# Expert routing spread over more steps, its table lookup moved from GpSimd to VectorE, and the low weight parts given to one engine per stage

## The chip, the cores and the metric

The program runs on 1 core of one Trainium2 chip. The metric is device time in microseconds (us) of one execution; less is better. TensorE does the matrix products, VectorE and GpSimd elementwise work, ScalarE activations and casts, and SyncE's queue issues nearly all DMAs.

## The reference

Three networks run one after the other on 256 positions of width 1024, all in float32. The change lies in the first network alone, in its two product-key expert layers (`peer_ffn`), cut here to what is computed:

```python
def peer_ffn(h, wq, k1, k2, u_tab, v_tab):
    def block(xb):                                   # 128 positions
        q = (xb @ wq).reshape(PEER_BLOCK, PEER_HEADS, 2, PEER_HALF)
        s1 = jnp.einsum('phd,kd->phk', q[:, :, 0], k1).astype(jnp.float32)
        s2 = jnp.einsum('phd,kd->phk', q[:, :, 1], k2).astype(jnp.float32)
        v1, i1 = lax.top_k(s1, PEER_TOPK)            # 16 of 128 keys
        v2, i2 = lax.top_k(s2, PEER_TOPK)
        cand = (v1[..., :, None] + v2[..., None, :]) # 256 sums per head
        cand_id = i1[..., :, None] * N_KEYS + i2[..., None, :]
        top_s, top_pos = lax.top_k(cand, PEER_TOPK)
        eid = jnp.take_along_axis(cand_id, top_pos, axis=-1)
        g = jax.nn.softmax(top_s, axis=-1)
        act = jax.nn.gelu(jnp.einsum('pd,phkd->phk', xb, u_tab[eid]))
        return jnp.einsum('phk,phkd->pd', g.astype(xb.dtype) * act, v_tab[eid])
    return lax.map(block, h.reshape(-1, PEER_BLOCK, D)).reshape(B, S, D)
```

There are 8 heads, 128 keys per half and so 16384 experts. The kernel gathers no expert rows. It multiplies all positions by the whole of U (128 chunks of 128 experts), builds a dense gate matrix G from the routing, and multiplies gelu(U h) times G by the whole of V.

## The kernel before

**Low parts.** Each float32 weight tile is split into a high part (rounded, ScalarE, line 164) and a low part (tile minus high part, line 168), and each product is three matmuls: high by high, high by low, low by high (`mm3`, lines 179 to 181). The third one needs the low part. `wunit` loads 512 KB into a `raw` buffer (6 of them), and writes both parts into the buffers `hl` (8 of them, so four tiles in flight in this stage). Its argument `lo` says who makes the low part: "v" is VectorE, "g" is GpSimd. Without an argument it follows the letters of `self.pat`.

**`peer_route`** runs once for each layer. It first multiplies by `wq`, eight groups of two tiles: three in `lead` together with the norm, then five in a loop that calls `advance(2.5)` before each. `ev_q` and `keys` make the key scores. Then `LAG + SPILL` = 91 chunks of U follow, each by one call of `step`: `advance(budget)`, then `u_chunk` (24 matmuls into one PSUM tile, then a gelu on ScalarE, line 1258), then the delayed products of the gate matrix. The first 40 activations are written to HBM, 51 stay in the `act` buffers (52).

**Routing** is a generator, `routing()`: 32 calls of `top_half` (VectorE's top-8 instructions over 128 scores, for 8 heads, 2 halves and 2 position blocks), then `route(th)` for each block of 128 positions. `route` adds the two lists to 54 candidates, takes the best 16 (lines 1107 to 1111), makes the softmax (an Exp on ScalarE, line 1117), turns positions into two indices A and B (lines 1125 to 1150), and looks both up in the index lists: a one-hot comparison `oh` (line 1157), a product with the list on GpSimd (line 1161) and a sum (line 1163), four times for each block. After three transposes on TensorE (line 1169) come 16 steps that build one-hot tiles `ob` (line 1184) and weighted ones `oa` (line 1190); TensorE multiplies these (line 1200, 16 products for each step), ScalarE evacuates (line 1204), and SyncE stores 1 MB of G (line 1207) for every two steps. The tiles `tr` that `ob` and `oa` read have two buffers, one block's worth; `ob` and `oa` have three each.

**Pacing.** Each `yield` of the generator gives the cost of what it has just emitted, and `advance` runs it until the costs have used up the budget. With the costs before, routing's last piece falls on step 64 of the 91; with those after, on step 83 (added up from the yields and budgets in the code). In what order an engine gets its instructions is settled when the program is built: a scheduler places the instructions in program order where they are ready by its own estimate, and may place a later one in a gap. On the chip each engine's order is then fixed.

**Who makes U's low parts.** Before: GpSimd for three chunks of every five, with the larger budget (2.6), else VectorE (1.5).

**`peer_value`** runs the other 37 chunks of U beside the products with V. Its first one needs `gr`, a read of G (line 1295) behind all its stores, then a product on GpSimd (line 1305).

Of the kernel before, what the change touches and what calls it, by code (L numbers as in the profile page):

```python
# [10 lines left out]
F32 = mybir.dt.float32  # L11
F32R = mybir.dt.float32r
BF16 = mybir.dt.bfloat16
F16 = mybir.dt.float16
# [6 lines left out]
P = 128  # L21
# [8 lines left out]
LAG = 51  # L30
SPILL = 40
# [21 lines left out]
MIX_BG = (0, 2, 4, 6, 8, 8)  # L53
MODS = ((1, 0, 2), (4, 3), (5,))
OH_COST = 1.3
BUDGET = (1.5, 2.6)
PAT_MIX = "ggv"
LEAD_LO = "vg"
SQ_POOL = 4
# [48 lines left out]
class Kern:  # L108
# [935 lines left out]
    def peer_route(self, l, nm):  # L1044
        hs = nm.xs
        nc, a = self.nc, self.a
        v = nc.vector
# [22 lines left out]
        def top_half(hd, s):  # L1070
            for th in range(2):
                for sd in range(2):
                    sj = s[:, th * 2 + sd]
                    Vt, It = V[th][sd], I[th][sd]
                    w = self.t([P, P], F32, "r")
                    v.max(out=Vt[:, hd, 0:8], in_=sj)
                    v.max_index(It[:, hd, 0:8], Vt[:, hd, 0:8], sj)
                    v.match_replace(w, Vt[:, hd, 0:8], sj, -3.0e38)
                    v.max(out=Vt[:, hd, 8:16], in_=w)
                    v.max_index(It[:, hd, 8:16], Vt[:, hd, 8:16], w)  # L1080
                    yield 1.0


        self.n += 1
# [3 lines left out]
        def route(th):  # L1088
            V1, V2 = V[th]
            If = []  # L1090
            for sd in range(2):
                t = self.t([P, 8, 16], F32, "r")
                v.tensor_copy(t, I[th][sd])
                If.append(t)
            cand = self.t([P, 8, 54], F32, "cand")
# [8 lines left out]
            for hd in range(8):  # L1104
                c = cand[:, hd]
                w = self.t([P, 54], F32, "r")
                v.max(out=TS[:, hd, 0:8], in_=c)
                v.max_index(PI[:, hd, 0:8], TS[:, hd, 0:8], c)
                v.match_replace(w, TS[:, hd, 0:8], c, -3.0e38)
                v.max(out=TS[:, hd, 8:16], in_=w)  # L1110
                v.max_index(PI[:, hd, 8:16], TS[:, hd, 8:16], w)
                if hd % 2:
                    yield 1.2

            g = self.t([P, 8, 16], F32, "r")
            v.tensor_sub(g, TS, TS[:, :, 0:1].broadcast_to([P, 8, 16]))
# [20 lines left out]
            v.tensor_scalar(u2, p, 37.0, None, op0=ALU.is_ge)  # L1137
            stt(u2, p, 40.0, u2, op0=ALU.is_ge, op1=ALU.add)
            stt(u2, p, 43.0, u2, op0=ALU.is_ge, op1=ALU.add)
            yield 1.2  # L1140
            stt(B, e16, -16.0, p, op0=ALU.mult, op1=ALU.add)
            stt(B, e24, -8.0, B, op0=ALU.mult, op1=ALU.add)
            stt(B, u1, -5.0, B, op0=ALU.mult, op1=ALU.add)
# [4 lines left out]
            v.tensor_add(A, A, e24)  # L1148
            v.tensor_add(A, A, u1)
            v.tensor_add(A, A, u2)  # L1150
            yield 1.8
            res = []
            for sel, tab in ((A, If[0]), (B, If[1])):
                ids = self.t([P, P], F32, "r")
                for hf in range(2):
                    oh = self.t([P, 4, 16, 16], BF16, "oh")
                    v.tensor_tensor(
                        oh.rearrange("p h k j -> p (h k) j"),
                        sel[:, hf * 64:hf * 64 + 64, None].broadcast_to([P, 64, 16]),
                        self.iota[:, None, 0:16].broadcast_to([P, 64, 16]), op=ALU.is_equal)  # L1160
                    nc.gpsimd.tensor_mul(oh, oh, tab[:, hf * 4:hf * 4 + 4, None, :].broadcast_to([P, 4, 16, 16]))
                    yield 1.1
                    v.tensor_reduce(ids[:, hf * 64:hf * 64 + 64], oh.rearrange("p h k j -> p (h k) j"),
                                    axis=AX.X, op=ALU.add)
                    yield 1.1
                res.append(ids)
            pt = self.ps("acc")
            for i, src in enumerate((g.rearrange("p h k -> p (h k)"), res[0], res[1])):
# [42 lines left out]
        def routing():  # L1211
            for s_hd in range(8):
                yield from top_half(s_hd, ss.pop(s_hd))
            for th in range(2):
                yield from route(th)

        ss = {}
        pend = []
        late = [[]]
        gen = routing()  # L1220
# [2 lines left out]
        def advance(budget):  # L1223
            self.debt += budget
            while self.debt > 0:
                try:
                    self.debt -= next(gen)
                except StopIteration:
                    return False
            return True  # L1230
# [4 lines left out]
        ss[1] = keys(1)  # L1235
        if LEADS > 2:
            ss[2] = keys(2)
        for g in range(LEADS, 8):
            advance(2.5)
            self.lin(wq, [g], hs, ev_q)  # L1240
            ss[g] = keys(g)

        acts = {}
        uw = {}
        st = {"u": 0}

        def u_chunk():
            i = st["u"]
            if i >= P:
                return  # L1250
            st["u"] += 1
            w = self.wload(a["U"][l, i // 2][:, (i % 2) * D:(i % 2) * D + D], NK, P,
                           lo="g" if i < LAG + SPILL and i % 5 < 3 else "v")
            p = self.ps()
            for k in range(NK):
                self.mm3(p[:, :S], *w[k], *hs[k], k == 0, k == NK - 1)
            t = self.t([P, S], F32, "act")
            nc.scalar.activation(t, p[:, :S], AF.Gelu_apprx_tanh)
            if i < SPILL:
                nc.sync.dma_start(Sd[i], t)  # L1260
            else:
                acts[i] = t
# [8 lines left out]
            return more or bool(pend) or any(late)  # L1271

        for i in range(LAG + SPILL):
            step(BUDGET[i % 5 < 3])
        while step(4.0):
            pass

        return u_chunk, acts, Gd, Sd

# [906 lines left out]
```

## Time and profile before

| | us |
|---|---|
| median of 3 runs | 3950.95 |
| lowest and highest run | 3948.46 and 3953.46 |
| the profiled execution's own time | 3954.35 |
| its span in the profile | 3952.5 |
| its mean granted TensorE clock | 0.97 |

The profiled execution is 3.4 us longer than the median of the runs shown, and 1.85 us of it lie outside the span. The engines' busy times over the span are 3712.5 us for TensorE's matmuls, 2832.6 us for VectorE, 1915.8 us for ScalarE and 1226.6 us for GpSimd. The two stages that the change touches begin with `wq` at about 200 and 1220 us; their 91 chunks of U run from about 248 to 594 us and from about 1268 to 1614 us. The page of the profile has a strip of 40 slices, about 99 us each, in which each digit is a busy share in tenths.

### The profile page before, as it was taken

The page shows a single profiled execution, that of the slowest core. Times are in us where ns is not written, and L with a number is a line of the kernel's source. Part 1 is how long each engine was busy: PE and PEld are TensorE (multiplying, and loading weights), DVE is VectorE, ACT ScalarE, POOL GpSimd, SP SyncE. Part 2 cuts the span into 40 slices and gives each one's busy share as a digit, 9 for nine tenths or more (in the row PEclk, how much of TensorE's full clock was granted, in tenths as well). Part 3 has the DMA queues.
Part 4 walks back from the last instruction along what each step waited for, and adds up shares of the span by engine and source line. Part 5 has one row for each costly group of instructions (what it writes and reads, how often), then busy time and mean ns, then how long its engine had stood idle before and what let it go on. Part 6 is the DMA issues. An engine that isn't in the chain of part 4 may idle for free.

```text
span 3952.5 us, 75873 instructions
## 1 busy us (share of the span) xinstructions
PE 3712.5 (94%) x30282; PEld 3626.1 (92%) x30282; DVE 2832.6 (72%) x5231; ACT 1915.8 (48%) x2900; POOL 1226.6 (31%) x922
## 2 busy tenths in 40 slices
PE   5888999999989799999999979999999998899998
PEld 4787999999979799999999979999899998789998
DVE  7899746676868976555667687675876768967665
ACT  4444544444454355444444434444554445755453
POOL 3335462133432545312424661121221212501100
PEclk8898999999999899999999989999999999999999
DMA  7545667796733477767764534558444553444452
GB/s 248 200 145 185 250 240 268 259 316 232 260 132 126 134 266 252 243 209 259 246 211 172 192 117 144 187 177 234 157 162 178 182 183 120 157 171 166 160 202 93
DMA packets 288435, 774.48 MB, mean 196 GB/s; under 512 B 25296, under 2 KB 117968, under 8 KB 283984
## 3 DMA queue, kind: packets, MB, share of 16 engines
q1 hardware_dynamic: 286496, 767.82, 56.7%
q8 instruction: 237, 3.88, 0.4%
q10 hardware_dynamic: 1584, 1.81, 0.1%
q14 instruction: 118, 0.97, 0.1%
HBM read 721.20 MB, written 48.27 MB: 195 GB/s over the span
## 4 chain that ended last, share of the span: by engine, by line
PE 65%; DVE 14%; DMA 2%; issue 2%; ACT 2%; POOL 1%; DVEq 0%; ACTq 0%; POOLq 0%; SPq 0%
PE mm L179 11%; PE mm L181 11%; PE mm L180 11%; PE acc L180 9%; PE acc L179 9%; PE acc L181 9%; DVE hl L168 2%; DMA raw<-in_ada 1%; DVE act L1399 1%; DVE hx L168 1%; DVE oa L1190 1%; DMA raw<-in_fg 1%; DVE M L1831 1%; DVE ob L1184 1%; DVE t L1739 1%
## 5 line engine op out<-in xcount | busy, mean ns | idle before, releaser
L168 DVE TENSOR_TENSOR hl<-raw,hl 128x512 fp32r<-128x512 f32 (+1 forms) x962 | 974.7, 1026 | 595.8 <-ACT hl L164 594.7
L164 ACT CAST hl<-raw 128x1024 fp32r<-128x1024 f32 x860 | 901.2, 1049 | 889.2 <-PE acc L180 396.2
L181 PE MATMUL mm<-h,hl 128*128 128x256 f32 x3688 | 1056.5, 287 | 60.4 <-POOL hl L168 32.2
L179 PE MATMUL mm<-h,hl 128*128 128x256 f32 x3688 | 1066.4, 289 | 1.6 <-DVE act L1859 1.2
L180 PE MATMUL mm<-h,hl 128*128 128x256 f32 x3688 | 1053.4, 286 | 0.3
L181 PEld LDWEIGHTS mm<-h,hl 128*128 128x128 f32 x3688 | 713.7, 194 | 67.5 <-POOL hl L168 34.4
L179 PEld LDWEIGHTS mm<-h,hl 128*128 128x128 f32 x3688 | 714.7, 194 | 5.7 <-issue 2.6
L180 PEld LDWEIGHTS mm<-h,hl 128*128 128x128 f32 x3688 | 714.5, 194 | 1.3 <-DVE h L586 0.9
L168 POOL TENSOR_TENSOR hl<-raw,hl 128x1024 fp32r<-128x1024 f32 x164 | 434.6, 2658 | 498.6 <-ACT hl L164 457.5
L181 PE MATMUL acc<-cc,hl 128*128 128x256 f32 x2048 | 579.2, 283 | 2.1 <-DVE hl L168 2.0
L179 PE MATMUL acc<-cc,hl 128*128 128x256 f32 x2048 | 578.9, 283 | 0.5 <-DVE x L1288 0.5
L180 PE MATMUL acc<-cc,hl 128*128 128x256 f32 x2048 | 579.0, 283 | 0.0
L168 DVE TENSOR_TENSOR hx<-raw,hx 128x512 fp32r<-128x512 f32 x558 | 425.4, 780 | 116.1 <-ACT hx L164 113.1
L1305 POOL TENSOR_TENSOR t<-act,gr 128x256 f32<-128x256 f32 x256 | 281.4, 1132 | 575.2 <-DMA gr<-G 465.7
L179 PE MATMUL mm<-h,hx 128*128 128x256 f32 x1464 | 415.6, 284 | 0.4 <-ACT hx L164 0.4
L181 PE MATMUL mm<-h,hx 128*128 128x256 f32 x1464 | 412.3, 282 | 0.8 <-POOL hx L168 0.6
L180 PE MATMUL mm<-h,hx 128*128 128x256 f32 x1464 | 412.9, 282 | 0.0
L164 ACT CAST hx<-raw 128x1024 fp32r<-128x1024 f32 x314 | 328.7, 1047 | 147.4 <-PE mm L180 73.5
L181 PEld LDWEIGHTS acc<-cc,hl 128*128 128x128 f32 x2048 | 389.7, 190 | 2.7 <-DVE hl L168 2.7
L179 PEld LDWEIGHTS acc<-cc,hl 128*128 128x128 f32 x2048 | 389.9, 190 | 0.7 <-DVE x L1288 0.7
L180 PEld LDWEIGHTS acc<-cc,hl 128*128 128x128 f32 x2048 | 389.7, 190 | 0.0
L754 POOL TENSOR_TENSOR t<-t,act 128x256 f32<-128x256 f32 x110 | 115.4, 1049 | 680.5 <-DVE t L753 641.0
(494 smaller groups left out, 7323.7 us busy)
## 6 DMA issues: line engine op xcount, KB each, us to landing
raw<-in_fg SPq DMA_DIRECT2D x264, 512.0 KB, 4.4
raw<-in_U SPq DMA_DIRECT2D x256, 512.0 KB, 4.5
raw<-in_V SPq DMA_DIRECT2D x256, 512.0 KB, 4.4
raw<-in_fd SPq DMA_DIRECT2D x132, 512.0 KB, 4.1
raw<-in_w SPq DMA_DIRECT2D x88, 512.0 KB, 4.0
G<-s SPq DMA_DIRECT2D x32, 1024.0 KB, 6.5
gr<-G SPq DMA_DIRECT2D x32, 1024.0 KB, 8.0
mr<-in_ada SPq DMA_DIRECT2D x56, 512.0 KB, 5.8
```

The costliest lines, as they stand in the source:

```text
L164: nc.scalar.copy(hi, raw)
L168: (nc.gpsimd if lo == "g" else nc.vector).tensor_sub(w, rw, h.bitcast(F32))
L179: mm(out, lhsT=wh, rhs=xh, start=start, stop=False, **kw)
L180: mm(out, lhsT=wh, rhs=xl, start=False, stop=False, **kw)
L181: return mm(out, lhsT=wl, rhs=xh, start=False, stop=stop, **kw)
L754: nc.gpsimd.tensor_mul(pr, u, r)
L1184: v.tensor_tensor(oh, self.iota2[:, None].broadcast_to([P, 8, P, 2]), ids[:, b].rearrange("p s (q u) -> p (s q) u", u=2)[:, :, None].broad ...
L1190: v.tensor_tensor(wo[:, 4 * z:4 * z + 4], oh[:, 0:4], w[:, b, z].rearrange("p (q u) -> p q u", u=2)[:, :, None].broadcast_to(shape), op=AL ...
L1305: nc.gpsimd.tensor_mul(c.rearrange("p (g t) -> p g t", g=16), act.rearrange("p (g t) -> p g t", g=16), gr[0][:, :, i % 8, :])
L1399: v.scalar_tensor_tensor(acc, q[:, j:j + S], w, acc, op0=ALU.mult, op1=ALU.add)
L1739: v.scalar_tensor_tensor(acc[:, sh:], p[:, 0:S - sh], w(i), acc[:, sh:], op0=ALU.mult, op1=ALU.add)
L1831: v.tensor_scalar(M[:, j, o:o + P], ab[:, j, i0:i0 + P], rt[:, b, h:h + 1], 0.0, op0=ALU.subtract, op1=ALU.min)
```

## The change

Four things, all in `peer_route`. The yields and budgets get other numbers (`BUDGET`, `yield`, `advance(4.2)`). The lookup's product (line 1161) goes from GpSimd to VectorE, with `oh` in float16 in place of bfloat16 and the lists converted to float16 in place of float32. U's low parts are GpSimd's while the generator is still in `top_half`, and VectorE's from the step in which `route` begins (`st["lo"]`). The five `wq` groups of the loop make their low parts by `PAT_Q` = "gv", the first of the two tiles of a group on GpSimd and the second on VectorE.

```diff
-BUDGET = (1.5, 2.6)
+BUDGET = (2.0, 2.7)
+PAT_Q = "gv"
...
                     v.max_index(It[:, hd, 8:16], Vt[:, hd, 8:16], w)
-                    yield 1.0
+                    yield 1.7
...
-                t = self.t([P, 8, 16], F32, "r")
+                t = self.t([P, P], F32, "r").bitcast(F16)[:, 0:P].rearrange("p (h k) -> p h k", h=8)
                 v.tensor_copy(t, I[th][sd])
...
                 if hd % 2:
-                    yield 1.2
+                    yield 2.5
...
-            yield 1.2
+            yield 2.0
             stt(B, e16, -16.0, p, op0=ALU.mult, op1=ALU.add)
...
-            yield 1.8
+            yield 3.0
             res = []
...
-                    oh = self.t([P, 4, 16, 16], BF16, "oh")
+                    oh = self.t([P, 4, 16, 16], F16, "oh")
...
-                    nc.gpsimd.tensor_mul(oh, oh, tab[:, hf * 4:hf * 4 + 4, None, :].broadcast_to([P, 4, 16, 16]))
-                    yield 1.1
+                    v.tensor_mul(oh, oh, tab[:, hf * 4:hf * 4 + 4, None, :].broadcast_to([P, 4, 16, 16]))
+                    yield 1.9
                     v.tensor_reduce(ids[:, hf * 64:hf * 64 + 64], oh.rearrange("p h k j -> p (h k) j"),
                                     axis=AX.X, op=ALU.add)
-                    yield 1.1
+                    yield 1.2
...
                 yield from top_half(s_hd, ss.pop(s_hd))
+
+            st["lo"] = "v"
             for th in range(2):
...
+        st = {"lo": "g"}
...
+        self.pat, self.upos = PAT_Q, 0
         for g in range(LEADS, 8):
-            advance(2.5)
+            advance(4.2)
             self.lin(wq, [g], hs, ev_q)
             ss[g] = keys(g)
+        self.pat = "v"
...
             w = self.wload(a["U"][l, i // 2][:, (i % 2) * D:(i % 2) * D + D], NK, P,
-                           lo="g" if i < LAG + SPILL and i % 5 < 3 else "v")
+                           lo=st["lo"])
...
-            step(BUDGET[i % 5 < 3])
+            step(BUDGET[st["lo"] == "g"])
         while step(4.0):
             pass
+        st["lo"] = "v"
```

## Rows read from the trace of the kernel before

**Rows 1.** The page's 40 slices: TensorE's busy tenths and its granted clock.

```profile
PE   5888999999989799999999979999999998899998
...
PEclk8898999999999899999999989999999999999999
```

**Rows 2.** Windows: us; PE, PEld, DVE, ACT, POOL busy; clock, DMA share, GB/s.

```profile
248.00:594.00 346.00, 313.36 (x2721) 308.60 (x2722) 265.31 (x433) 159.95 (x261) 188.13 (x82) 0.95 0.61 214
1268.00:1614.00 346.00, 312.43 (x2735) 307.08 (x2734) 266.66 (x446) 161.48 (x263) 189.34 (x82) 0.96 0.61 214
...
360.00:380.00 20.00, 16.48 (x149) 16.02 (x148) 19.90 (x14) 8.52 (x15) 10.30 (x4) 0.83 0.89 312
660.00:1060.00 400.00, 397.24 (x3302) 396.18 (x3301) 271.99 (x316) 186.35 (x275) 110.75 (x102) 1.00 0.80 269
```

**Rows 3.** TensorE's waits, 248 to 594 us: total us, times, longest.

```profile
PE mm L181 <- POOL hl L168: 14.8, 4, 6.3
PE mm L181 <- DVE hl L168: 10.8, 5, 3.9
PE acc L1200 <- DVE oa L1190: 6.0, 8, 2.5
```

**Rows 4.** TensorE's timeline from 345.9 us: start, us, instruction.

```profile
345.97 0.28 PE L181 MATMUL mm<-h,hl 128*128 128x256 f32 x1
346.09 1.09 PE L1200 MATMUL acc<-oa,ob 128*128 128x128 f16 x16
346.98 0.36 PE L179 MATMUL mm<-h,hl 128*128 128x256 f32 x1
```

**Rows 5.** VectorE's groups by shape, 248 to 594 us.

```profile
L1190 DVE TENSOR_TENSOR oa<-ob,tr 128x1024 f16<-128x1024 f16 x64 | 74.9, 1213 | 0.9
L168 DVE TENSOR_TENSOR hl<-raw,hl 128x1024 fp32r<-128x1024 f32 x40 | 67.5, 1696 | 65.1 <-ACT hl L164 65.1
L1184 DVE TENSOR_TENSOR ob<-vec,tr 128x2048 f16<-128x2048 f16 x32 | 52.3, 1639 | 0.0
```

**Rows 6.** GpSimd's groups in the same stretch.

```profile
L168 POOL TENSOR_TENSOR hl<-raw,hl 128x1024 fp32r<-128x1024 f32 x53 | 144.0, 2727 | 124.4 <-ACT hl L164 124.4
L1161 POOL TENSOR_TENSOR oh<-oh,r 128x1024 bf16<-128x1024 bf16 x8 | 25.4, 3189 | 27.6 <-DVE oh L1157 27.6
```

**Rows 7.** VectorE's timeline from 254.7 us.

```profile
254.75 0.30 DVE L1076 MAX8 r<-c2p 128x8 f32<-128x128 f32 x1
254.95 0.30 DVE L1079 MAX8 r<-r 128x8 f32<-128x128 f32 x1
255.14 2.96 DVE L168 TENSOR_TENSOR hl<-raw,hl 128x1024 fp32r<-128x1024 f32 x1
```

**Rows 8.** GpSimd's timeline in that stretch.

```profile
254.62 2.40 POOL L168 TENSOR_TENSOR hl<-raw,hl 128x1024 fp32r<-128x1024 f32 x1 [5.94 <-ACT hl L164]
257.50 2.87 POOL L168 TENSOR_TENSOR hl<-raw,hl 128x1024 fp32r<-128x1024 f32 x1 [0.48 <-ACT hl L164]
```

**Rows 9.** VectorE's timeline while GpSimd is idle.

```profile
509.24 1.21 DVE L1184 TENSOR_TENSOR ob<-vec,tr 128x2048 f16<-128x2048 f16 x1
...
511.70 1.22 DVE L1184 TENSOR_TENSOR ob<-vec,tr 128x2048 f16<-128x2048 f16 x1
...
514.16 2.35 DVE L168 TENSOR_TENSOR hl<-raw,hl 128x1024 fp32r<-128x1024 f32 x2
```

**Rows 10.** Instructions of a tile or line: ns min/median/max, first and last start.

```profile
L1190 DVE TENSOR_TENSOR oa<-ob,tr x128: 676/691/2949, 331.9 to 1533.5; 128x1024 f16<-128x1024 f16 x128
...
L168 POOL TENSOR_TENSOR hl<-raw,hl x164: 2337/2442/3691, 18.6 to 3721.9; 128x1024 fp32r<-128x1024 f32 x164
```

**Rows 11.** ScalarE's timeline at the first Exp.

```profile
275.38 0.31 ACT L1117 ACTIVATE r<-r 128x128 f32<-128x128 f32 x1 [3.16 <-DVE r L1116]
```

**Rows 12.** SyncE's, then GpSimd's timeline where the second routing ends.

```profile
1543.90 0.38 SPq L1207 DMA_DIRECT2D G<-s  x1
...
1555.95 0.74 POOL L1305 TENSOR_TENSOR t<-act,gr 128x256 f32<-128x256 f32 x1 [8.66 <-DMA gr<-G]
```

More of the change, by code (lines that the diff above doesn't have):

```diff
@@ L1237, in peer_route @@
             ss[2] = keys(2)
+        self.pat, self.upos = PAT_Q, 0
         for g in range(LEADS, 8):
-            advance(2.5)
+            advance(4.2)
             self.lin(wq, [g], hs, ev_q)
             ss[g] = keys(g)
+        self.pat = "v"
         acts = {}
         uw = {}
-        st = {"u": 0}
+        st["u"] = 0
         def u_chunk():
```

## The prediction

> **What bounds the kernel now.** I read the 40 slices first. TensorE is busy nine tenths or more nearly everywhere at full clock; counted from 0, slice 3 (296 to 395 us) and slice 13 (1284 to 1383 us), where both strips dip to 8 and to 7 and 8, lie in the two routing stages [rows 1]. The windows put sizes to them: over the 91 chunks of U in each stage, 346 us long, TensorE's granted clock averages 0.95 and 0.96 and VectorE is busy 265 us; in a stretch of the V stage of 400 us, where VectorE makes all low parts, the clock is 1.00 and TensorE is busy 397 us [rows 2].
>
> The waits name the cause: 14.8 us for low parts from GpSimd, 10.8 us for those from VectorE, 6.0 us for `oa` [rows 3], 31.6 us in all. The clock adds to that: 0.05 of 346 us is 17 us of full-speed work, since TensorE runs at 1.2 in place of 2.4 GHz for a while behind a long wait (0.83 over 360 to 380 us, [rows 2]). So a stage loses about 49 us; with 0.96 and the same waits the second loses 45. A count of the work checks it: matmuls start 0.12 us apart and a routing step of 16 products takes 0.89 us [rows 4], so 91 x 24 x 0.12 + 32 x 0.89 = 290.5 us of 346, which leaves 55. I take 49 + 45 = 94 us as what there is to win, with 110 as the other bound.
>
> Why the low parts are late is in the two timelines laid side by side. GpSimd's low part starts at 254.62 and ends at 257.02; VectorE's, started at 255.14, takes 2.96 us, and GpSimd's next one 2.87 in place of 2.40 [rows 7, 8]. With GpSimd idle the same VectorE instruction takes 1.18 us [rows 9]. The top-8 instructions are unharmed: 0.30 us, 0.20 apart, inside GpSimd's instruction [rows 7]. So VectorE's subtractions and products stand still while GpSimd works, and GpSimd is held up too (2.73 us on average against a median of 2.44 over the whole program, [rows 6, 10]). One sentence in the Trainium skill, page SBUF — State Buffer, section Who interferes with whom, says this: an instruction with two SBUF inputs on VectorE and one on GpSimd that reads SBUF exclude each other for their whole length, and a VectorE instruction with at most one, outside its two-port modes, does not contend; the trace agrees with 2.96 us and 0.30 us.
>
> **The change part by part, for one stage.**
>
> Low parts. VectorE now makes those of chunks 12 to 90 (routing enters `route` on the thirteenth step: 19 top-k pieces are left after `wq`, 32.3 of cost at 2.7 a step), 79 in place of 36 (two of five): +43 x 1.18 = +51 us of VectorE.
>
> The lookup product. GpSimd loses 8 x 3.19 us [rows 6]. VectorE gains 8 such products. The trace has none there; the nearest row is `oa`, float16 inputs and output of the same size, 0.69 us [rows 10], and the bound above is the float32 subtraction of that size, 1.18 [rows 9]. I take 0.69: +5.5 us (9.4 by the bound).
>
> The stalls that go. With GpSimd idle from about chunk 12 to the end of routing, `oa` falls from 1.213 to 0.69 (64 x 0.52 = 33 us), the low parts from 1.70 to 1.18 (40 x 0.52 = 21), `ob` from 1.64 to 1.21 (32 x 0.43 = 14) [rows 5, 9, 10]: -68 us. In all VectorE has 265 + 51 + 5.5 - 68 = 254 us to do beside TensorE's 290: 87%, and it has to be even.
>
> Is it even? In a step with `ob` and `oa`: an `ob` with its two `oa` takes 2.46 us (509.24 to 511.70, [rows 9]); the budget of 2.0 buys 2.0/2.6 of it, 1.89 us, and the low part 1.18: 3.07 us. TensorE has 2.88 + 0.77 x 0.89 = 3.57. In the 31 steps before the `ob` of both blocks the costs are the listed durations, at most 2.0 + 1.18 = 3.18 against 2.88; but small instructions start 0.20 apart where 0.30 is listed [rows 7], so nearer 2.0 x 2/3 + 1.18 = 2.5. Excess 0 to 31 x 0.30 = 9 us; I take 0. Before, the same budgets were 1.5 and 2.6 with the stalls on top.
>
> The first 12 chunks. GpSimd makes all low parts, 2.44 us each against TensorE's 2.88. VectorE has none there, and any work of `route` that is ordered early meets GpSimd. If each GpSimd part took the 3.69 us of the slowest one [rows 10], 12 x 0.81 = 10 us would be lost. Low parts of chunk 12 and after may also come late behind that work, with four tiles in flight to cover it. Range 0 to 10; I take 5.
>
> The two Exps. ScalarE stood 3.16 us for the softmax's input with its casts queued behind [rows 11]. Nothing in the change orders that otherwise. Two of these, 0 to 6.3 us; I take 2, as four tiles hold 11 us of TensorE's work.
>
> The `wq` loop. Its five first tiles go to GpSimd, and five VectorE parts (5.9 us) leave VectorE. TensorE is full there, so there is nothing to gain; cost taken as nothing, hidden by two tiles (5.76 us of TensorE) for each group.
>
> The start of V. Routing's last piece falls on step 83, not 64, and its products two steps later, so chunks 86 to 90 are left, 14.4 us, to cover the store of G, its read and the first product. From the store's issue to GpSimd's first product it was 12.05 us [rows 12]; with the evacuation and queue ahead of it and the cast and subtraction behind, I estimate 17. The wait of 2.6 us, with the clock's share (49/31.6 = 1.55), costs 4; bounds 0 and 10 (17 us with half the cover). SyncE's queue issues the loads of U behind the read of G and has six buffers ahead.
>
> Uneven VectorE work in the rest: 2, with its upper bound among the rivals.
>
> Sum: 5 + 2 + 4 + 2 = 13 us stay lost in each stage; 94 - 26 = 68 us are won. 3954.35 - 68 = 3886; the profiled execution lies 3.4 us above the median, so 3883 against 3950.95. The count of the work leaves up to 16 us more to win; for a small part of that I say 3881.
>
> **The rivals.**
>
> Slower: 79 chunks in place of 36 get their low part from the in-order engine that also routes. TensorE waited 10.8 us for 36 such parts, 0.30 each [rows 3]. If each of the 79 waits 0.6 us behind a burst of routing, that is 47 us of waits, 73 with the clock, 24 to 28 more than is lost now in each stage: 4003. It decides from 0.39 us for each part (47/1.55/79). For it: 87% load. Against: in the V stage VectorE is busy 272 of 400 us and TensorE loses 3 us [rows 2]. 7%.
>
> Partly given back: the waits for each VectorE part stay at 0.30 us although the stalls go. 79 x 0.30 x 1.55 = 37 us lost, 10 a stage won: 3931. For it: the scheduler's order is made without knowing the real times. Against: the waits fell where the stalls were. 18% for 3906 to 3942.
>
> The lock in the `wq` loop: with tiles taking turns, each VectorE part waits for GpSimd's whole instruction, 2.44 us. If all five reached TensorE, 5 x 2.44 x 1.55 = 19 us a stage: 3919. The skill's sentence quoted above makes such waits possible; the profile has nothing of this in the loop, where one engine made both. 4%.
>
> No effect: the order on each engine is the scheduler's; where it had filled VectorE's gaps with routing anyway, new budgets move little, and a later start of V takes the rest. 4%.
>
> Transfers as the bound: a stage moves 214 GB/s x 346 us = 74 MB; over 300 us that is 247 GB/s, and 312 were reached [rows 2]. It is below 1%, and I leave it out.
>
> **How the numbers follow.** The likeliest case, 67%, is 3844 to 3905: nothing lost at all at one end (110 us won), all bounds above reached together at the other (5 + 4 + 6 + 8 us a stage more, rounded). Its far ends are unlikely, so the range for 8 in 10 starts at 3853 and reaches into the cases partly given back, to 3919. A difference under 0.2% (8 us) can't be told from none here. Faster: 0.67 + 0.18 + 0.04 = 0.89; the same 0.04; slower 0.07.
>
> **What would show it.** Right: over the chunks of U the clock is 0.98 or more; `oa` and low parts on VectorE have means near 0.7 and 1.2 us; GpSimd shows no instruction between its last low part and the first product with G; the first V product comes some 30 to 40 us sooner after the first chunk. Wrong: waits of TensorE for VectorE's parts of more than 20 us a stage (the order), for GpSimd's in the first 12 chunks (the lock), or a gap ahead of the first V product (the late end of routing) over 10 us.

## The result, and the profile after

| | before | after |
|---|---|---|
| median of the runs on one chip | 3950.41 us | 3899.43 us (3894.93 to 3901.57, 4 runs) |
| ratio | | 0.9864, interval 0.9848 to 0.988 |
| profiled execution: time, granted clock | 3954.35 us, 0.97 | 3901.57 us, 0.975 |

The kernel became 1.4% faster: 51 us where 70 were forecast. Where the 52.8 us between the two profiled executions come from is read at four points: the first product with V (the first `acc<-cc` matmul) and the end of each V stage (the first addition to `x` on VectorE).

| us from the start | before | after | won by then |
|---|---|---|---|
| layer 0, first product with V | 594.3 | 566.0 | 28.3 |
| layer 0, end of V | 1064.2 | 1046.5 | 17.7 |
| layer 1, first product with V | 1614.4 | 1563.5 | 50.9 |
| layer 1, end of V | 2079.8 | 2032.2 | 47.6 |

So the first routing stage wins 28.3 us, the V stage behind it gives 10.6 back (469.9 us become 480.5), the second wins some 33, and its V stage gives 3.3 back. The last 5 us lie behind the second layer, where nothing was changed: from there to the end it takes 1872.6 us before and 1867.6 after, and in the fourteen profiled executions of this document between 1860.3 and 1873.5. So those 5 us are no more than executions differ by anyway, and the two layers themselves account for 47.6.

The slices of the page, TensorE's busy tenths and its clock: of the dips of [rows 1] in the routing stages (8 busy in slices 2 and 3, 7 in slice 13, with a clock of 8 in 3 and 13) an 8 in slice 13 is left, and the clock is 9 throughout there.

```profile
PE   5899999999989899999999979999999998899998
...
PEclk8999999999989999999999989999999999999999
```

Windows over the chunks of U in the two stages, to be laid beside [rows 2]; the columns are the same:

```profile
248.00:566.00 318.00, 304.39 (x2737) 301.77 (x2736) 247.63 (x454) 158.91 (x257) 25.73 (x13) 0.98 0.66 226
1248.00:1564.00 316.00, 305.96 (x2773) 303.50 (x2772) 253.51 (x482) 162.18 (x263) 29.83 (x16) 0.98 0.67 230
```

The stage of the first layer is 28 us shorter, the clock rose from 0.95 to 0.98, GpSimd went from 188 us to 26, and VectorE, although it makes twice the low parts, from 265 to 248. VectorE's groups by shape in the first of them, against [rows 5], with the new lookup product as the last row:

```profile
L169 DVE TENSOR_TENSOR hl<-raw,hl 128x1024 fp32r<-128x1024 f32 x82 | 99.6, 1223 | 62.7 <-ACT hl L165 62.7
L1191 DVE TENSOR_TENSOR oa<-ob,tr 128x1024 f16<-128x1024 f16 x64 | 41.2, 687 | 0.8
L1185 DVE TENSOR_TENSOR ob<-vec,tr 128x2048 f16<-128x2048 f16 x32 | 38.8, 1218 | 0.0
...
L1162 DVE TENSOR_TENSOR oh<-oh,r 128x1024 f16<-128x1024 f16 x8 | 5.3, 684 | 0.0
```

The stalls are gone: `oa` 1.213 to 0.687 us, the low part 1.70 to 1.22, `ob` 1.64 to 1.22. TensorE's waits there, against [rows 3]:

```profile
PE mm L182 <- DVE hl L169: 10.1, 2, 7.2
PE mm L182 <- POOL hl L169: 2.1, 1, 2.1
PE acc L1201 <- ACT act L1264: 1.0, 1, 1.0
```

31.6 us of waits have become 14. Most of what remains is one place, the switch, where the low parts pass from GpSimd to VectorE (7.2 of VectorE's 10.1 us and all of GpSimd's; the other 2.9 us fall at 358.45, where the first `ob` and `oa` are made). These are windows of TensorE from 260 us:

```profile
260.00:280.00 20.00, 17.43 (x127) 17.02 (x127) 20.00 (x87) 8.18 (x12) 10.87 (x5) 0.87 0.44 139
280.00:300.00 20.00, 12.83 (x90) 12.63 (x90) 19.96 (x43) 6.47 (x10) 2.84 (x2) 0.84 0.34 117
300.00:320.00 20.00, 20.00 (x161) 20.00 (x160) 19.76 (x81) 10.73 (x15) 0.00 (x0) 0.95 0.63 204
```

A full window counts 169 matmuls; 42, 79 and 8 are missing, 129 x 0.12 = 15.5 us. The second layer loses the same at 1268 to 1328 us (121, 90 and 168 matmuls). What happens there is read from GpSimd's timeline first, then from VectorE's (only its long rows), then from ScalarE's and TensorE's:

```profile
262.02 2.40 POOL L169 TENSOR_TENSOR hl<-raw,hl 128x1024 fp32r<-128x1024 f32 x1 [0.48 <-ACT hl L165]
272.96 7.41 POOL L169 TENSOR_TENSOR hl<-raw,hl 128x1024 fp32r<-128x1024 f32 x3 [8.54 <-ACT hl L165]
281.38 2.47 POOL L169 TENSOR_TENSOR hl<-raw,hl 128x1024 fp32r<-128x1024 f32 x1 [1.00 <-ACT hl L165]
```

```profile
256.33 2.42 DVE L1094 CAST r<-r 128x128 f16<-128x128 uint32 x1
...
258.87 0.20 DVE L1094 CAST r<-r 128x128 f16<-128x128 uint32 x1
...
273.18 2.44 DVE L1143 SCALAR_TENSOR_TENSOR r<-r,r 128x128 f32<-128x128 f32 x1
...
281.51 2.49 DVE L1150 TENSOR_TENSOR r<-r,r 128x128 f32<-128x128 f32 x1
284.37 2.36 DVE L1158 TENSOR_TENSOR oh<-r,vec 128x1024 f16<-128x1024 f32 x2
...
295.84 1.21 DVE L169 TENSOR_TENSOR hl<-raw,hl 128x1024 fp32r<-128x1024 f32 x1
```

```profile
271.64 0.31 ACT L1118 ACTIVATE r<-r 128x128 f32<-128x128 f32 x1 [5.21 <-DVE r L1117]
```

```profile
275.52 0.58 PE L182 MATMUL mm<-h,hl 128*128 128x256 f32 x1 [2.08 <-POOL hl L169]
297.10 0.58 PE L182 MATMUL mm<-h,hl 128*128 128x256 f32 x1 [7.17 <-DVE hl L169]
```

VectorE begins `route` with the casts of the index lists (L1094), the first of them at 256.33, while GpSimd still has low parts to make. The first cast and many of its two-input instructions take 2.4 us each there, as long as GpSimd's own; the second cast takes 0.20 us at 258.87, in GpSimd's pause. The softmax's input is late for it, ScalarE stands 5.21 us for it with its own casts (the high parts) behind, and so GpSimd's last four parts fall after 272.96, where they hold VectorE once more (L1143 to L1150). Four lookups follow in one run, and only then, at 295.84, comes the first low part of VectorE's, for which TensorE has waited 7.17 us.

The other loss is in the V stage, and its greater part at the start. SyncE's last store and first read of G, four windows behind the first product, and one farther on:

```profile
550.16 0.33 SPq L1208 DMA_DIRECT2D G<-s  x1
555.02 0.59 SPq L1302 DMA_DIRECT2D gr<-G  x1
```

```profile
580.00:600.00 20.00, 18.81 (x157) 18.60 (x156) 12.48 (x14) 8.31 (x13) 12.91 (x13) 1.00 0.87 298
600.00:620.00 20.00, 17.59 (x145) 17.19 (x143) 12.93 (x16) 9.14 (x14) 5.33 (x5) 1.00 0.85 268
620.00:640.00 20.00, 19.21 (x158) 19.01 (x159) 11.76 (x16) 8.05 (x12) 3.42 (x4) 1.00 0.69 238
640.00:660.00 20.00, 17.57 (x145) 17.17 (x144) 13.65 (x16) 8.05 (x12) 5.90 (x6) 1.00 0.90 285
...
700.00:720.00 20.00, 17.96 (x135) 17.76 (x136) 14.44 (x16) 7.45 (x12) 9.72 (x8) 0.91 0.88 294
```

169 fit; before the change each of the five had 169. Before, the first read of G was issued 64 us ahead of the first product (530.3 and 594.3), now 11. VectorE stands in order for background loads of `ada` (the weights of a later modulation), with V's low parts behind them:

```profile
615.93 1.28 DVE L839 CUSTOM_DVE_ANT_0 raw<-raw,vec 128x1024 f32<-128x1024 f32 x1 [7.07 <-DMA raw<-in_ada]
```

Before, the longest such wait of the stage was 4.5 us. In sum VectorE waits little longer than it did: from 566 to 1060 us 78.9 us for these loads, where it was 76.8 before. What is new is that three loads issued at 591 to 606 us, among the late reads of G, landed 8.5 to 9.9 us after their issue; before, none of the stage's 32 took more than 5.9. The changed kernel's second run shows such a load too, 9.9 us.

### The profile page after: what moved, and what is told of

It is laid out like the page before. It is cut to its first block, busy times and chain, and to the rows that moved or that the text cites. A ratio compares the mean times of both kernels' runs of the same rounds, so it can differ in the third digit from the quotient of the medians.

```text
span 3899.8 us, 75836 instructions
## 1 busy us (share of the span) xinstructions
PE 3694.3 (95%) x30282; PEld 3608.6 (93%) x30282; DVE 2809.2 (72%) x5323; ACT 1916.5 (49%) x2900; POOL 959.0 (25%) x830
## 4 chain that ended last, share of the span: by engine, by line
PE 76%; DVE 16%; DMA 4%; issue 2%; ACT 2%; POOL 0%; DVEq 0%; ACTq 0%; SPq 0%; POOLq 0%
PE mm L180 14%; PE mm L182 14%; PE mm L181 14%; PE acc L181 10%; PE acc L180 10%; PE acc L182 10%; DVE hl L169 2%; PE acc L1201 1%; DMA raw<-in_ada 1%; DVE ld L450 1%; DMA S<-act 1%; DVE M L1838 1%; DVE hx L169 1%; DVE mr L839 1%; DMA raw<-in_fg 1%
## 5 line engine op out<-in xcount | busy, mean ns | idle before, releaser
L169 DVE TENSOR_TENSOR hl<-raw,hl 128x512 fp32r<-128x512 f32 (+1 forms) x1038 | 1035.3, 1010 | 580.7 <-ACT hl L165 576.0
L180 PEld LDWEIGHTS mm<-h,hl 128*128 128x128 f32 x3688 | 708.5, 192 | 10.8 <-issue 4.5
L169 POOL TENSOR_TENSOR hl<-raw,hl 128x1024 fp32r<-128x1024 f32 x88 | 220.4, 2513 | 269.4 <-ACT hl L165 228.2
```

The costliest lines, as they stand in the source:

```text
L169: (nc.gpsimd if lo == "g" else nc.vector).tensor_sub(w, rw, h.bitcast(F32))
L180: mm(out, lhsT=wh, rhs=xh, start=start, stop=False, **kw)
```

## The experiments

All ratios are against the kernel before on the same chip. The table sets the kernels beside each other; the V stage and the lead of G's first read are of layer 0, from one profiled execution each; two executions of the changed kernel differ by 2 us in the V stage (480.5 and 478.7), so smaller differences say nothing.

| kernel | ratio (interval) | first product with V | V stage | read of G ahead |
|---|---|---|---|---|
| before | 1 | 594.3 | 469.9 | 64 |
| lookup alone | 0.9951 (0.9935 to 0.9968) | 584.7 | 476.6 | 64 |
| pacing alone | 0.9961 (0.995 to 0.9973) | 593.2 | 472.0 | 46 |
| low-part policy alone | 0.9847 (0.9831 to 0.9864) | 561.6 | 469.3 | 63 |
| the change | 0.9864 (0.9848 to 0.988), again 0.9875 (0.9861 to 0.9889) | 566.0 | 480.5 | 11 |
| the change, GpSimd out | 0.9844 (0.9827 to 0.986) | 561.6 | 473.7 | 8 |
| the change, `ada` late | 0.9943 (0.9928 to 0.9958) | 567.9 | 498.3 | 11 |
| the change, `ada` from position 10 | 0.9869 (0.9853 to 0.9886) | 567.2 | 488.1 | 11 |
| the change, budget 2.4 | 0.985 (0.9837 to 0.9863) | 566.1 | 469.8 | 43 |
| the change, old `wq` loop | 0.9852 (0.9836 to 0.9867) | 564.3 | 482.2 | 11 |
| the change, old top-8 rate | 0.983 (0.9816 to 0.9843) | 556.0 | 477.1 | 25 |
| policy + lookup | 0.9807 (0.9794 to 0.982) | 557.7 | 474.0 | 63 |
| policy + lookup, GpSimd out | 0.9787 (0.9772 to 0.9802) | 548.9 | 469.6 | 63 |

**The parts alone.** The lookup product on VectorE, on top of the kernel before:

```diff
-                    oh = self.t([P, 4, 16, 16], BF16, "oh")
+                    oh = self.t([P, 4, 16, 16], F16, "oh")
-                    nc.gpsimd.tensor_mul(oh, oh, ...)
+                    v.tensor_mul(oh, oh, ...)
```

> The kernel before with the lookup's product alone moved to VectorE (float16), everything else as before. Theory A (VectorE and GpSimd stand still for each other, above all over the low parts): 53 low parts of a stage stay on GpSimd, so VectorE's one-hot tiles and low parts stay slow (means near 1.2 and 1.7 us); 5 to 25 us are won, 3925 to 3945. Theory B (the products stand ahead of low parts in GpSimd's queue, and that makes the low parts late): TensorE's 14.8 us of waits for GpSimd's parts go in each stage, with the clock some 23 us each, so about 3905. Theory C (pacing): no change, 3945 to 3955.

Measured: 3937.66 us, 18.6 won. Its waits of TensorE:

```profile
PE mm L181 <- DVE hl L168: 16.4, 5, 9.3
PE acc L1200 <- DVE oa L1190: 9.7, 12, 5.0
PE mm L181 <- POOL hl L168: 2.6, 1, 2.6
```

The wait for GpSimd's parts falls from 14.8 to 2.6 us, but those for VectorE's rise (10.8 to 16.4, and 6.0 to 9.7 for `oa`): VectorE is still held by GpSimd's low parts (`oa` 1.11 us, low part 1.67). Time and means are theory A's; that GpSimd's parts were waited for less is theory B's.

The policy of the low parts alone, with the lookup product left on GpSimd:

```diff
+            st["lo"] = "v"          # between top_half and route
-                           lo="g" if i < LAG + SPILL and i % 5 < 3 else "v")
+                           lo=st["lo"])
```

> The kernel before with the low parts alone changed: GpSimd makes U's while the generator is in the top-k pieces, VectorE after that; yields, budgets, lookup and wq as before. Theory A: most of the 51 us is here, 30 to 50 won, 3900 to 3920, and the one-hot tiles' mean falls to about 0.7 us. Theory B: GpSimd's queue holds the products alone and VectorE waits for them as before; 10 to 25 won. Theory C: VectorE has more to do at the old uneven pace, so nothing is won or some lost, 3945 to 3975.

Measured: 3894.68 us, 61.6 won, more than expected and as much as the whole change. `oa` takes 0.697 us, the low part 1.34. GpSimd's eight lookup products take 4.1 us each beside a busy VectorE, and still nothing waits long for them.

The pacing alone (the costs that `yield` hands back, the `wq` loop's budget and the steps' budgets):

```diff
-BUDGET = (1.5, 2.6)
+BUDGET = (2.0, 2.7)
-                    yield 1.0
+                    yield 1.7
-            advance(2.5)
+            advance(4.2)
```

> The kernel before with the new yields and budgets alone; low parts by threes of five on GpSimd and the lookup on GpSimd as before. Theory A: within 12 us of before, 3938 to 3962, as the two engines still meet. Theory C (routing came in bursts faster than VectorE can work): at least half of the gain, 25 us or more, 3925 or less, with TensorE's waits for VectorE's parts halved from 10.8 us a stage.

Measured: 3940.1 us, 16 won by the clock, but only 4.4 of them by the end of layer 1's V stage; the rest lies where nothing was changed. The waits don't fall: 14.8 us for GpSimd's parts, 10.7 for VectorE's, and 9.1 for `oa`, where it was 6.0. So the pacing alone hardly makes the routing stage faster.

**Is the wait at the switch GpSimd's lock** (VectorE standing still while GpSimd works)**?** The change with VectorE making every low part from the `wq` loop on (`PAT_Q = "v"`, `st = {"lo": "v"}`), GpSimd none:

> The changed kernel with all low parts of the stage on VectorE, those of the first 12 chunks and of the wq loop too, so GpSimd does nothing before the first product with G. What is tested is the wait that is left in the changed kernel where VectorE takes over (7.2 and 7.3 us for its first low part). Theory A1 (VectorE is 15 us behind its order there, because it stood still behind GpSimd's low parts in the first 12 chunks): the wait goes, and 10 to 25 us are won against the changed kernel, 3875 to 3890. Theory A2 (the order itself puts the four lookups in one run ahead of that low part): a wait of 5 us or more stays and the 17 more low parts cost VectorE 20 us a stage in its fullest stretch: 3895 to 3930.

Measured: 3895.11 us. The windows at the switch are full:

```profile
260.00:280.00 20.00, 20.00 (x169) 20.00 (x169) 20.00 (x115) 7.94 (x13) 0.00 (x0) 1.00 0.65 214
280.00:300.00 20.00, 19.08 (x160) 18.88 (x159) 19.86 (x45) 10.73 (x16) 0.00 (x0) 1.00 0.68 203
```

So in this kernel it is the lock: theory A1's wait goes. Its time doesn't come; 3895.11 us lies at the edge of theory A2's range, and the ratio's interval overlaps that of the changed kernel's first runs. At the gelu of chunk 80 the kernel is 19.3 us ahead of the changed one (511.2 against 530.5 us), at the first product with V only 4.4. Routing ends no sooner (its last store of G goes out at 549.2 us, in the changed kernel at 550.2), G's first read goes out at 554.12, and the first product with V waits for its operand:

```profile
561.65 0.80 PE L180 MATMUL acc<-cc,hl 128*128 128x256 f32 x2 [5.07 <-ACT cc L203]
```

The windows behind it lose matmuls too. What was won at the switch is mostly lost again where G comes late.

**Why does the V stage give time back?** The changed kernel again, as the yardstick, and on the same chip two kernels with one edit each.

> The changed kernel itself, as the yardstick of this chip. Both theories expect 0.986 of the kernel before (0.9848 to 0.988 was measured), a first V product near 566 us, a V stage of layer 0 near 480 us (470 before) and one wait of about 7 us for VectorE's low part where the low parts pass from GpSimd to VectorE.

Measured: 3906.18 us, 0.9875; V stage of layer 0 478.7 us, wait at the switch 9.9. The loss repeats.

```diff
-            if pos % 4:
+            if pos >= 40 and pos % 4:
                 bg(1)
```

> The changed kernel with the background loads of ada held back until position 40 of the V stage (before: from position 1). Theory A: VectorE stands in order for these loads (waits of 7.1 and 6.3 us at 616 and 600 us) with V's low parts behind it, and this is what the V stage of layer 0 gives back; then without them at its start the stage takes 470 to 474 us in place of 480.6, the windows from 580 to 660 us are full, and the kernel gains 6 to 10 us on the changed one. Theory B: the reads of G that come late, after the later end of routing, take the DMA time at the start of V; then the stage stays at 478 to 483 us and the gain is under 3 us.

Measured: 3931.84 us, 26 slower than the changed kernel, 20 of them in layer 0's V stage. Two of its windows by 40 us:

```profile
600.00:640.00 40.00, 40.00 (x336) 40.00 (x335) 20.91 (x21) 18.48 (x28) 6.77 (x7) 1.00 0.59 191
...
880.00:920.00 40.00, 37.45 (x306) 36.64 (x305) 33.77 (x42) 19.05 (x29) 17.46 (x16) 1.00 0.92 320
```

The start of V is now full, 336 matmuls in every 40 us up to 760, with G read as late as in the changed kernel: the late reads of G alone don't hurt it. But the loss has moved, not gone. From about 770 us U's chunks are used up and a product takes 24 x 0.12 = 2.88 us; each needs 512 KB of V, 182 GB/s, and an `ada` load at three products of four makes it 319. The windows there show 302 to 320 GB/s at a DMA share of 0.9, and V's weights come late: ScalarE waits for them up to 6.8 us, VectorE up to 5.2 for ScalarE's casts, TensorE up to 7.9 for low parts.

```diff
-BUDGET = (2.0, 2.7)
+BUDGET = (2.4, 2.7)
```

> The changed kernel with a budget of 2.4 in place of 2.0 for each step of routing where VectorE makes the low parts, so routing ends about 12 steps sooner (71 steps of 142/2.4 = 59 after the switch, in place of 83) and G is read some 40 us sooner before V. Theory B (late G reads cost the V stage): the V stage of layer 0 falls to 470 to 474 us, and the wait at the switch stays near 7 us; gain on the changed kernel 5 to 10 us. Theory A (ada loads): the V stage stays within 3 us of 480. Theory C, the rate sets the load: VectorE has 2.4/2.0 more routing a step, 0.4 us more against TensorE's 3.57 us, and TensorE's waits for VectorE's low parts in the routing stage rise from 10 us to over 20, so that the first V product comes later than 566.

Measured: 3893.78 us, 12 better than the changed kernel on that chip. The V stage takes 469.8 us with the `ada` loads where they were, the start of V is full, and the wait at the switch stays (9.9):

```profile
580.00:600.00 20.00, 20.00 (x169) 20.00 (x168) 11.24 (x14) 9.41 (x14) 2.02 (x3) 1.00 0.88 288
600.00:620.00 20.00, 20.00 (x169) 20.00 (x168) 15.31 (x17) 9.38 (x14) 8.75 (x6) 1.00 0.77 261
```

Theory B's numbers are met (the stage a little below its range, the gain 2 us above), and theory C's are not: the first product with V comes at 566.1 us as in the changed kernel, so VectorE's higher rate costs TensorE nothing. So the start of V is full if the `ada` loads are away, and also if they stay and routing ends sooner. To see whether it is their meeting with the late G that costs, the loads were put off by ten positions only:

```diff
-            if pos % 4:
+            if pos >= 10:
                 bg(1)
```

> The changed kernel with the background loads of ada held until position 10 of the V stage and then one at every position (they were three in four from position 1), so that 28 of the 32 run while U's chunks still take half of TensorE's time: two chunks of 512 KB and an ada load in 5.76 us are 273 GB/s, below the 302 to 320 at which the kernel that held them to position 40 came late. Theory A (the loads at V's start, where the late reads of G are, cost what the V stage gave back): windows from 580 to 620 us full at 169 matmuls, V stage of layer 0 at 470 to 474 us in place of 479 to 481, 6 to 10 us better than the changed kernel, 0.984 to 0.985. Theory B (VectorE stands for these loads wherever they lie, and what it costs depends on how many there are in a stretch): the loss moves behind position 10, the windows from 620 us on fall under 160, the V stage stays at 477 to 483 us, 0.986 to 0.988.

Measured: 3904.57 us, 0.9869. Four of its windows:

```profile
580.00:600.00 20.00, 20.00 (x169) 20.00 (x168) 13.06 (x10) 9.22 (x15) 15.38 (x15) 1.00 1.06 360
600.00:620.00 20.00, 20.00 (x169) 20.00 (x169) 12.68 (x12) 9.25 (x15) 8.94 (x8) 1.00 0.62 200
...
680.00:700.00 20.00, 16.75 (x135) 16.14 (x135) 12.84 (x16) 6.83 (x11) 0.65 (x1) 1.00 0.81 259
...
740.00:760.00 20.00, 17.65 (x143) 17.04 (x142) 12.70 (x14) 7.76 (x12) 8.15 (x8) 1.00 0.94 316
```

The start of V is full, as theory A said, but its time doesn't come: the loss now lies at 680 to 800 us, 100 us behind the late reads of G, and it is larger (V stage 488.1 us, where theory A had said 470 to 474 and theory B 477 to 483). In the window with 135 matmuls the transfers ran at 259 GB/s, less than in full windows, so their rate alone doesn't explain it. TensorE waits for VectorE's low parts, 15 times in the stage's products with U and 1.6 us at most, with VectorE standing 24 times for `ada`, up to 5.2 us.

The edit changed two things, the place of the loads and their rate (four in four positions in place of three), and no run makes this move at the old rate. Nor is VectorE's standing for these loads the measure of the loss: from 566 to 1060 us it comes to 76.8 us in the kernel before, 78.9 in the changed one, 73.8 with the budget of 2.4 and 66.7 here, where the loss is largest. So for the start of V the runs show that it takes both, the loads and a late end of routing: it is full without either. What stays open is why loads farther on (700 to 720 us in the changed kernel, 680 to 800 here) cost matmuls, when the same loads cost next to nothing where routing ends sooner.

**What the pacing costs.** On the chip of the yardstick: the policy and the lookup product on the kernel before, with its pacing and its `wq` loop:

> The kernel before with the policy of the low parts and the lookup product on VectorE, and the old pacing and the old wq loop. The policy alone had given 0.9847, all of the change's gain. Theory D (the new pacing is what costs: VectorE has room, and the slower rate only moves the end of routing into V): 0.980 to 0.983, first V product at 556 to 561 us. Theory E (the lookup product on VectorE is what costs, since the engine that makes all low parts gets 5.5 us more in runs of four): 0.986 to 0.988 as the changed kernel, with a wait over 5 us at the switch and a first V product at 563 to 568 us.

Measured: 3880.57 us, 25.6 better than the changed kernel, whose interval its own doesn't touch. Theory D's ratio and first product with V (557.7 us) are met. SyncE's first read of G and a window:

```profile
494.95 0.59 SPq L1298 DMA_DIRECT2D gr<-G  x1
```

```profile
260.00:280.00 20.00, 13.94 (x106) 13.53 (x106) 19.90 (x107) 8.99 (x13) 2.75 (x2) 0.88 0.32 103
280.00:300.00 20.00, 20.00 (x161) 20.00 (x161) 20.00 (x36) 8.30 (x13) 0.00 (x0) 0.95 0.81 258
```

G is read 60 us sooner, and the switch costs 63 + 8 = 71 matmuls, 8.5 us in place of 15.5. The top-8 pieces say why. The last instruction of them starts at 260.8 us here and at 259.1 in the changed kernel, although a piece costs 1.0 here and 1.7 there: its five instructions start 0.20 us apart, with three short loads of 0.06 us between them, so a piece takes about 1.2 us, nearer to 1.0 than to 1.7. VectorE runs through them at its own speed; the higher cost only lets more chunks of U into the top-k stage, 12 for GpSimd in place of 8, and the last four are those that come after 272.96.

The same, with GpSimd out of U altogether (`st = {"lo": "v"}`):

> The low-part policy and the lookup product on VectorE with the old pacing and the old wq loop (0.9807), and besides VectorE makes the low parts from the first chunk of U, GpSimd none. Theory A: what was still lost around the switch (106 matmuls in the window 260 to 280 us where 169 fit, 63 x 0.12 = 8 us, in each layer) came from VectorE's instructions standing while GpSimd works; without GpSimd that window has 160 or more, and the kernel gains 10 to 16 us: 0.9766 to 0.9782. Theory B: VectorE is busy the whole of 220 to 280 us with top-8, so eight more low parts (8 x 1.18 = 9.4 us) push routing back as much as the stalls did; gain under 4 us, 0.980 to 0.982.

Measured: 3870.34 us, the lowest of all. By the ratios the gain is 8 us, between the two theories; the interval holds theory A's upper end, 0.9782, and theory B's lower end, 0.980, and it overlaps that of the kernel without this edit, so the gain isn't clear of noise. In the profiled executions the first product with V comes 8.8 us sooner, of which 4.0 are there already when the first top-8 starts (208.6 and 212.6 us); from there to the end of the V stage the two layers together gain 11.4 us, within theory A's 10 to 16. One window I had wrong: the loss at the switch is hardly smaller, 64 matmuls in place of 71, and moved back.

```profile
260.00:280.00 20.00, 18.98 (x156) 18.57 (x155) 20.00 (x114) 9.25 (x14) 0.00 (x0) 1.00 0.64 190
280.00:300.00 20.00, 16.23 (x118) 15.29 (x117) 19.96 (x36) 9.60 (x15) 0.00 (x0) 0.91 0.53 165
```

VectorE is busy for the whole of both, with GpSimd idle; ScalarE's wait for the softmax's input is 1.2 us in place of 5.9. So the lock isn't all there is at the switch: with the old pacing VectorE's own work is too dense there, while the changed kernel with GpSimd out, which differs from this one in the pacing alone, has full windows.

That pair also gives the price of the pacing by itself: 0.9844 with the new costs (0.9827 to 0.986), 0.9787 with the old (0.9772 to 0.9802), each against the kernel before on its own chip.

The change with the old `wq` loop (`PAT_Q = "v"`):

> The changed kernel with VectorE making all low parts of the wq loop, as before the change. Theory P (the lock in the wq loop costs nothing that TensorE sees beyond 153 and 164 matmuls where 166 fit, 1.8 us a layer): within 0.001 of the changed kernel's 0.9875. Theory Q (VectorE's parts there wait for GpSimd's whole instruction, and top-8 comes later for it, so that the switch comes late too): 0.983 to 0.985, and the wait at the switch falls by half.

Measured: 3898.71 us, 0.9852, between the two theories, with an interval that overlaps the changed kernel's. At the switch it has 108 and 126 matmuls where the changed kernel has 127 and 90, a loss of 104 in place of 121. What GpSimd's five parts in the `wq` loop cost stays open; by the ratios it is 5 to 9 us, with overlapping intervals. From this kernel to the policy with the lookup (0.9807, 0.9794 to 0.982) only the pacing differs, and the intervals don't touch (0.9836 to 0.9867 here): the second pair in which the new pacing alone costs about half a per cent.

The change with the old top-8 rate (`yield 1.0`, `advance(2.5)`), the later costs and the budget of 2.0 as changed:

> The changed kernel with the cost of a top-8 piece back at 1.0 and the wq loop's budget back at 2.5; the new costs of the later routing pieces and the budget of 2.0 stay. Theory S (the top-8 piece was overrated: its instructions start 0.20 us apart, so VectorE is through with them before GpSimd's twelve low parts are, and enters the selection with the lock on): GpSimd makes 8 low parts in place of 12, none after 264 us, TensorE's wait at the switch falls from 7 to 10 us to about 3, first V product at 556 to 561 us, the V stage of layer 0 at 476 to 480 us, and 0.983 to 0.985. Theory R (the rate of the later pieces is the larger part: the end of routing stays late, step 79 in place of 83): first V product 562 us or later, V stage of layer 0 at 479 or more, 0.986 to 0.988.

Measured: 3887.42 us, 0.983. Theory S in its main numbers: GpSimd's last low part of U starts at 257.13, first product with V at 556.0, V stage 477.1 with G read 25 us ahead. The wait at the switch falls to 1.2 us, where about 3 was expected; the longest wait for a low part, 4.8 us, now comes at 328.9, where the first `ob` and `oa` are made. The distance from here to 0.9807 is left for the later pieces' rate and the `wq` loop together; the two intervals overlap.

## Why the prediction came out as it did

The time lies within the range, above the likeliest figure, and the mechanism was the right one; two terms were mis-sized.

**Right.** GpSimd's low parts held VectorE: the policy of the low parts alone gives the whole gain. The prices held: lookup product 0.69 forecast, 0.684 measured; `oa` 0.69 and 0.687; low part 1.18 and 1.22; `ob` 1.21 and 1.22; VectorE's work in the stage 254 us and 248. The clock of 0.98 came. Of the routing stages alone, 36 and 32 us were forecast (49 and 45 less 13), and 28 and 33 came; the 28 lies just under the sign I had named, 30 to 40 us. That some 94 us were there to win is borne out in the main: policy and lookup with GpSimd out win 42 in each routing stage.

**The first 12 chunks and the Exps**, taken at 5 + 2 us a stage with bounds of 10 + 6.3, measured 15.5: close to both bounds together. I had priced GpSimd's slowed low parts and said of VectorE only that early work of `route` would meet them. The step that misled me was that the top-8 instructions are unharmed. They are, but the work behind them is not: 128x128 instructions of `route` go from about 0.25 to 2.4 us, tenfold, each held for a whole instruction of GpSimd. The trace before had this already, beside three low parts of GpSimd (301.08 to 309.11 us):

```profile
304.46 4.74 DVE L1093 CAST r<-r 128x128 f32<-128x128 uint32 x2
```

The Exps' waits are 5.2 us in layer 0, all of it the first Exp's, within the bound of 6.3 but not at the 2 I took, and 8.1 + 3.0 us in layer 1, beyond it. They are not hidden by four tiles, because the tiles behind are those that GpSimd makes late.

**The start of V**, 4 us with bounds 0 and 10, was looked for at the wrong place. I took a wait ahead of the first product with V; there is none to speak of. The loss is 10.6 us inside the V stage of layer 0 and 3.3 in layer 1. The low parts that TensorE waits for there stand on VectorE behind the background loads of `ada`; 32 of the 40 such loads run in layer 0's V stage and 8 in layer 1's, which goes with the sizes of the two losses. A sooner end of routing takes the loss away, so the late end is its condition, as the term assumed; how the two act together is shown only in part (three loads that land late among the reads of G). The step that failed is what would be late next: I followed the store, the read and the first product of G, and in the changed kernel none of these is what TensorE waits for. With GpSimd out it is: there the wait of 5.07 us ahead of the first product with V is the one that I had looked for. The bound of 10 also left out the clock's share that the 4 has: 9.8 x 1.55 is 15.

**The pacing** had no term of its own; I took it as what makes VectorE's work even. The experiments show that it costs: about half a per cent in two pairs of kernels that differ in nothing else, 0.7% together with the `wq` loop. Part of it is the top-8 rate, where the evidence was in [rows 7]: instructions start 0.20 us apart, so that the old cost of 1.0 was nearer the truth; I used it only to find that VectorE had room. The rest goes with the late end of routing: the budget of 2.4, which ends it sooner, wins 12 us back. The pacing does even out VectorE's work at the switch, as I meant it to, but that shows only where GpSimd is out.

**The rivals.** None came true as told. The measured time is above the likeliest figure, but not for the reason of the case partly given back: the waits for VectorE's parts are two, not 0.30 us for each of 79. Transfers as the bound, below 1%, were met only in the V stage of the kernel that held `ada` to position 40.

**The range** has a slip in its sum. The upper end of the likeliest case, 3905, adds the 23 us of bounds once; for two stages it is 46, which from 3881 gives 3927, beyond the 3919 given as the range's end. The measured 3899 lies below either, so the slip decided nothing. With the two mis-sized terms as measured (15.5 for 7 in both layers, 10.6 and 3.3 for 4) the same sum gives 45 us won in place of 68, and 47.6 came by the end of the second layer. That the two terms stayed within the range is the width of the range, not a good estimate of either.

Open: how a late end of routing makes the `ada` loads cost beyond the start of V; a lead of G's first read is no full measure of it, since two kernels with 63 and 64 us of it lost 4 and 7 us in V (474.0 and 476.6).

## What to carry to other kernels

When work leaves an engine that holds another, ask where the two still overlap for a while: the loss collects there, at the switch, and small two-input instructions pay most. Give a pacing by costs the distance between starts that the trace shows, not the duration of an instruction; overrated work slides later and meets what comes next. A background load on which an in-order engine waits can be free for long (76.8 us of such waits cost little before the change) and cost once the work behind it has no time to spare. Here both ways of putting the loads off made the V stage longer; ending the work ahead sooner made it shorter.

## What the runs showed of the hardware

Beside GpSimd's 2.40 us subtraction, VectorE's CAST from 128x128 uint32 takes 2.42 us against 0.20 in GpSimd's pause, and its 128x128 instructions with two inputs 2.44 to 2.49 against 0.23 to 0.29, while GpSimd is hardly slowed (7.41 us for three). In [rows 8] a GpSimd part met by a 128x1024 subtraction of VectorE took 2.87. The other way round, GpSimd's bfloat16 lookup product takes 4.1 us when VectorE makes all low parts of that stretch and 3.19 in [rows 6]. Transfers reached 320 GB/s over 40 us at a DMA share of 0.92, where V's weights came late, and 360 over 20 us in a window in which TensorE was full. VectorE's small top-8 instructions, 0.28 to 0.30 us each, start 0.20 us apart.
